# Attention scores of two heads in three 64-row passes instead of four 128-row passes, with the queries left on their partitions

## The chip, the core and the metric

The kernel runs on one core of one Trainium2 chip. The metric is the device time of one launch in microseconds (us); lower is better. The engines named below are TensorE (PE, with its weight loads as PEld), VectorE (DVE), ScalarE (ACT), GpSimd (POOL) and SyncE (SP), which issues nearly all DMAs here.

## What is computed

Two token groups (512 and 256 tokens, 768 together, width 1024, fp32) pass through two layers with shared weights. Layer 0 mixes tokens by windowed attention, layer 1 by a gated convolution; each layer then has a squared-ReLU MLP and a gated embedding. The change is in the attention of layer 0:

```python
qkv = h @ w_qkv                        # 16 query heads, 4 key heads, 64 wide each
# for each block of 128 queries, keys of the blocks before, of and after it:
logits = jnp.einsum('bqgrd,bkgd->bgrqk', qb, kb,
                    preferred_element_type=jnp.float32) * scale + band_bias
m = jnp.maximum(jnp.max(logits, axis=-1, keepdims=True), sink_logit)
pexp = jnp.exp(logits - m)
probs = pexp / (jnp.sum(pexp, axis=-1, keepdims=True) + jnp.exp(sink_logit - m))
return jnp.einsum('bgrqk,bkgd->bqgrd', probs, vb)
```

A block at the edge of its token group has 2 key blocks (256 keys), an inner one 3 (384 keys). The 512-token group has blocks with 2, 3, 3 and 2 key blocks, the 256-token group two with 2. Four query heads share one key head.

## The kernel before

All products keep fp32 accuracy with a rounded format: each operand is split into a high part in fp32r (ACT copies it, L779) and a low part (DVE subtracts, L782), and a product is the sum of high x high, high x low and low x high. `product` (L735) does so for the projections with three 128-row matmuls for each block of 128 inputs.

The attention stage is `mixer_attention` (L668 to L1333). Nothing in it is issued at once. Each step becomes an operation with an engine, a cost in us, the operations it waits for (`after`) and the buffers it uses. `Plan.order` (L544) then makes a list schedule: on each engine it takes, among the operations that can start, the one with the longest path behind it; it repeats this and keeps the best order. The costs are constants such as `MM` (L664), 0.2275, 0.1743 and 0.12 us for a matmul of 512, 384 and 256 columns. The engines then run their queues in that order, and semaphores hold the true dependences. Rings of buffers are operations too: an operation that opens a buffer waits for the users of the one before it in the ring. The score banks (tag `S`) are a ring of three PSUM banks (`BS`, L30).

Queries are made in eight units of 128 columns, that is two heads each (`queries`, L1031). A unit multiplies its weights with the normed tokens, scales the result (L1000), splits it into `qh` and `ql` with the two heads on partitions 0 to 63 and 64 to 127, and then four DMAs on SP's queue (L1045, issued at L694) move the halves: the tile of a head, one of eight slots (`QS`, L675), gets the high part on its upper 64 partitions and the low part on its lower 64. The keys (`keys`, L1014) are moved likewise, so that `khh[g]` holds the high part of key head g on both halves and `kll[g]` the low part on both.

Then `attend` (L1128) handles one key head and one block of queries, 24 times in all. For each of its four heads it takes one score bank and does two matmuls (L1153, L1154) of 128 rows: the head's high and low queries, one above the other, against `khh` and against `kll`. That gives all four products of the parts in two passes. DVE adds the bias, takes the minimum (the scores are negated) and writes the logits out of the bank (L1160); ACT takes the exponential and its sum (L1170). After the reciprocal (L1176) the rows are scaled (L1183 on ACT, L1185 on DVE), turned by PE (L1196), split (L1205, L1206) and multiplied with the values (L1211), and the result is joined (L1220, L1227).

The four groups of heads (L1237) are planned among the units of queries, the projections, and the output product (L1260), which fill PE while an attention step waits for DVE and ACT.

Of the kernel before, what the change touches and what calls it, by code (L numbers as in the profile page):

```python
# [10 lines left out]
F32 = mybir.dt.float32  # L11
F32R = mybir.dt.float32r
AF = mybir.ActivationFunctionType
ALU = mybir.AluOpType
# [3 lines left out]
P = 128  # L18
# [4 lines left out]
HEADS, KV, HD = 16, 4, 64  # L23
REP = HEADS // KV
# [5 lines left out]
BM, BS, BO, BT, BL = 1, 3, 1, 2, 5  # L30
# [20 lines left out]
def trunk_kernel(ctx: ExitStack, tc: tile.TileContext, a: dict, out: bass.AP):  # L51
    nc = tc.nc
    act, dve, pe = nc.scalar, nc.vector, nc.tensor
# [19 lines left out]
    nsink = const.tile([P, HEADS], F32, name="nsink")  # L73
# [105 lines left out]
    class Norm:  # L179


        n = T
# [30 lines left out]
        ready = False  # L213
# [268 lines left out]
    class Plan:  # L482
# [12 lines left out]
        def op(self, engine, cost, run, after=(), uses=(), behind=(), lands=None):  # L495
            flat = []
            for d in after:
                flat.extend(d if isinstance(d, (list, tuple)) else [d])
            o = Op(engine, cost, run, [d for d in flat if d is not None], list(behind), lands)
            for key in uses:  # L500
                assert key not in self.closed, key
                self.users.setdefault(key, []).append(o)
                if key in self.opened and self.opened[key] not in o.after:
                    o.behind.append(self.opened[key])
            self.ops.append(o)
            o.bonus = self.bonus if engine == "PE" else 0.0
            return o

        def new(self, tag, bufs, make):

            box = Box()
            box.key, box.free = self.ring(tag, bufs)
            box.make, box.ahead, box.op = make, self.last.get(tag), None
            self.last[tag] = box
            return box

        def first(self, box, engine, cost, run, after=(), uses=(), lands=None):

            def start():
                box.t = box.make()  # L520
                run()

            behind = [box.ahead.op] if box.ahead is not None and box.ahead.op is not None else []
            box.op = self.op(engine, cost, start, [box.free, *after], [box.key, *uses], behind, lands)
            self.opened[box.key] = box.op
            return box.op
# [135 lines left out]
        return 0.067 + 0.00104 * n  # L662

    MM = {512: 0.2275, 384: 0.1743, 256: 0.12}  # L664

    psum = ctx.enter_context(tc.tile_pool(name="ps", bufs=1, space=PSUM))

    def mixer_attention():  # L668
# [4 lines left out]
        odd = s1.enter_context(tc.tile_pool(name="odd", bufs=2))  # L673

        KHI, KLO, QS = (0, 1, 4, 8), (2, 3, 5, 9), (6, 7, 14, 15, 10, 11, 12, 13)  # L675
        W0 = SEQS[0]
        LW = 3 * P + 1
        plan = Plan()
        op, new, first = plan.op, plan.new, plan.first

        def bank(tag, name="mm"):
            return new(tag, PB[tag], lambda: psum.tile([P, 512], F32, tag=tag, name=name, bufs=PB[tag]))

        def temp(tag, name, dt=F32):
            return new(tag, 3, lambda: tmp.tile([P, T], dt, tag=tag, name=name, bufs=3))

        def place(i, name, dt=F32R):
            return new(f"S{i}", 1, lambda: slot(i, name, dt))

        def dma(box, src, n, after=(), uses=(), queue="SP", rate=400e3):  # L690

            def run():
                d, s = src()
                (nc.sync if queue == "SP" else act).dma_start(d, s)  # L694

            lands = n / rate
            if box is not None and box.op is None:
                d = first(box, queue, 0.46, run, after, uses, lands)
            else:
                d = op(queue, 0.46, run, after, uses, lands=lands)  # L700
            d.kind = "move" if rate < 400e3 else None
            return d
# [64 lines left out]
        def halves(w, xs, tags, col=0, fine=False):  # L767

            o, out = 0, []
            for tag, n in zip(tags, SEQS):  # L770
                ps = bank(tag)
                out.append((ps, o, n, product(ps, w, xs, o, n, col, fine)))
                o += n
            return out
# [215 lines left out]
        tr = first(rt, "PE", 0.4, columns, [rstd], [r.key])  # L990
        rcs = first(rc, "DVE", 0.1, lambda: dve.tensor_copy(rc.t[:], rt.t[:, : T // P]), [tr], [rt.key])

        def scaled(ps, t, neg, tag):

            ops = []
            for i, (b, o, n, last) in enumerate(ps):

                def run(b=b, o=o, n=n):
                    if neg:
                        dve.scalar_tensor_tensor(  # L1000
                            t.t[:, o : o + n], b.t[:, :n], -(HD**-0.5), r.t[:, o : o + n], ALU.mult, ALU.mult
                        )
                    else:
                        dve.tensor_tensor(t.t[:, o : o + n], b.t[:, :n], r.t[:, o : o + n], ALU.mult)

                f = first if i == 0 else lambda _, *z: op(*z)
                ops.append(f(t, "DVE", V(n), run, [last, rstd], [b.key, r.key] + ([t.key] if i else [])))
            hi, lo = temp(tag, "qh", F32R), temp(tag, "ql", F32R)
            h, l = split_op(hi, lo, lambda: t.t, T, ops, [t.key])
            return (hi, h), (lo, l)  # L1010

# [17 lines left out]
                        dst.ready.append(dma(dst, ends, 196608, [ready], [part.key] + ([dst.key] if i else []), rate=215e3))  # L1029

        def queries(c, w, tags, tag):  # L1031
            parts = scaled(halves(w, xs, tags), temp(tag, "qt"), True, tag)
            for j in range(2):
                h = 2 * c + j
                dst = qst[h] = place(QS[h % 8], "q")
                dst.ready = []
                for i, (part, ready) in enumerate(parts):

                    def ends(dst=dst, part=part, i=i, j=j):
                        return (  # L1040
                            dst.t[64 * i : 64 * i + 64, :].bitcast(F32),
                            part.t[64 * j : 64 * j + 64, :].bitcast(F32),
                        )

                    dst.ready.append(dma(dst, ends, 196608, [ready], [part.key] + ([dst.key] if i else []), rate=215e3))  # L1045

        wq = [prepared(fetched(a["w_q"][0]), KB)]
        skewed = dma(
# [79 lines left out]
        def attend(g, n, lo_blk, hi_blk):  # L1128
# [6 lines left out]
            mn = new("mn", 2, lambda: odd.tile([P, REP], F32, name="mn"))  # L1135
            sm = new("sm", 2, lambda: odd.tile([P, REP], F32, name="sm"))
            lg, sums = [], []
            for h in range(REP):
                hp, j = divmod(h, 2)
                H_ = REP * g + h  # L1140
                if j == 0:
                    L = new("L", BL, lambda: odd.tile([P, 2 * LW], F32, tag="L", name="L", bufs=BL).rearrange(
                        "p (a b) -> p a b", a=2))
                    lg.append(L)
                    sunk = first(L, "POOL", 0.2, lambda L=L, H_=H_: nc.gpsimd.tensor_copy(
                        L.t[:, :, 0:1], nsink[:, H_ : H_ + 2].rearrange("p (a b) -> p a b", b=1)), [turned])
                L = lg[hp]
                S = bank("S", "S")

                def score(S=S, H_=H_):  # L1150
                    q = qst[H_].t[:, n * P : (n + 1) * P]
                    kk = slice(k0 * P, k0 * P + w)
                    pe.matmul(S.t[:, :w], lhsT=q, rhs=khh_[g].t[:, kk], start=True, stop=False)  # L1153
                    pe.matmul(S.t[:, :w], lhsT=q, rhs=kll_[g].t[:, kk], start=False, stop=True)  # L1154

                s = first(S, "PE", 0.24 if nk == 2 else 0.35, score,
                          [qst[H_].ready, khh[g].ready, kll[g].ready], [qst[H_].key, khh[g].key, kll[g].key])

                def reduced(S=S, L=L, j=j, h=h, H_=H_, hp=hp):
                    dve.tensor_tensor_reduce(  # L1160
                        L.t[:, j, 1 : 1 + w], S.t[:, :w], bias[hp].t[:, j, j0 : j0 + w], 1.0,
                        nsink[:, H_ : H_ + 1], ALU.add, ALU.min, accum_out=mn.t[:, h : h + 1],
                    )

                args = "DVE", 0.40 if nk == 2 else 0.53, reduced, [s, bias[hp].ready, sunk, turned]
                uses = [S.key, L.key, bias[hp].key]
                m = first(mn, *args, uses) if h == 0 else op(*args, [mn.key, *uses])

                def exponent(L=L, j=j, h=h):
                    act.activation(L.t[:, j, : 1 + w], L.t[:, j, : 1 + w], AF.Exp, bias=mn.t[:, h : h + 1], scale=-1.0,  # L1170
                                   accum_out=sm.t[:, h : h + 1])

                args = "ACT", 0.50 if nk == 2 else 0.61, exponent, [m, sunk]
                e = first(sm, *args, [mn.key, L.key]) if h == 0 else op(*args, [sm.key, mn.key, L.key])
                sums.append(e)
            rs = op("DVE", 0.09, lambda: dve.reciprocal(sm.t[:], sm.t[:]), [sums], [sm.key])  # L1176
            normed = []
            for h in range(REP):
# [1368 lines left out]
```

## Time and profile before

| | us |
|---|---|
| median of 3 runs | 1637.23 (1636.72 to 1637.66) |
| profiled execution, its own time | 1636.62 |
| span of the profile, first to last instruction | 1634.8 |
| PE busy | 1623.9 |
| weight loads (PEld) busy | 1573.5 |
| DVE busy | 1390.6 |
| ACT busy | 918.9 |
| first and last score matmul, from the span's start | 71.0 and 232.5 |

The granted clock of TensorE is 0.999 of full speed. Busy times are those of one profiled execution; a matmul's recorded duration contains its latency, and neighbours overlap, so the step from start to start says what it occupies. In a row of a group stand the line, engine, operation, output and inputs, the shape and the count; behind the bar the busy time in us, the mean of one in ns, and the idle time before it with what ended it. A timeline row has its start and its length in us; "x2" merges two instructions that follow each other.

### The profile page before, as it was taken

How to read it: one execution, taken by the hardware profiler on the slowest of the kernel's cores; microseconds unless marked ns; L12 is line 12 of the kernel's file. 1: busy time of each engine (PE TensorE's matmuls, PEld its weight loads, DVE VectorE, ACT ScalarE, POOL GpSimd, SP SyncE). 2: the span in 40 equal slices, each digit the busy share in tenths (PEclk: the TensorE clock that was granted, in tenths of full speed). 3: DMA queues.
4: the chain of work that ended last, by engine and by line, in shares of the span. 5: the costliest groups of instructions: out<-in, count | busy, mean ns of one | idle time of the engine just before them, and what ended most of it. 6: DMA issues, size and time to landing. Idle time of an engine off the chain costs nothing.

```text
span 1634.8 us, 24125 instructions
## 1 busy us (share of the span) xinstructions
PE 1623.9 (99%) x9371; PEld 1573.5 (96%) x9371; DVE 1390.6 (85%) x2214; ACT 918.9 (56%) x1454; POOL 11.1 (1%) x60
## 2 busy tenths in 40 slices
PE   9999999999999999999999999999999999999998
PEld 7988889999999999999999999999999999999987
DVE  7579988999999989977878778778989999999686
ACT  7478876656555555545654334555555555654455
POOL 0000000000000000000000000000000000000000
PEclk9999999999999999999999999999999999999999
DMA  8744312322212122222312222211222121222332
GB/s 304 201 122 136 120 37 84 104 73 70 75 68 78 66 77 78 75 87 75 116 62 65 69 74 77 78 52 65 65 78 78 65 78 67 76 69 74 116 98 90
DMA packets 47822, 144.80 MB, mean 89 GB/s; under 512 B 6075, under 2 KB 9531, under 8 KB 47708
## 3 DMA queue, kind: packets, MB, share of 16 engines
q1 hardware_dynamic: 47564, 143.14, 27.0%
q8 instruction: 73, 1.20, 0.3%
q14 instruction: 41, 0.34, 0.1%
q10 hardware_dynamic: 144, 0.13, 0.0%
HBM read 123.85 MB, written 9.96 MB: 82 GB/s over the span
## 4 chain that ended last, share of the span: by engine, by line
PE 96%; DVE 1%; DMA 1%; ACT 1%; issue 0%; SPq 0%; DVEq 0%
PE a L470 34%; PE b L470 8%; PE mm L747 8%; PE mm L137 8%; PE p L1560 6%; PE d L470 5%; PE c L470 5%; PE gate L137 4%; PE gate L1894 4%; PE B L470 4%; PE C L470 4%; PE down L1894 2%; PE O L1211 1%; PE pt L1196 1%; PE S L1153 1%; PE S L1154 1%
## 5 line engine op out<-in xcount | busy, mean ns | idle before, releaser
L438 ACT ACTIVATE whi<-sum 128x1024 fp32r<-128x1024 f32 x66 | 70.0, 1061 | 253.9 <-PE a L470 252.2
L470 PE MATMUL a<-xs,whi 128*128 128x384 f32 x608 | 117.7, 334 | 0.0
L470 PEld LDWEIGHTS a<-xs,whi 128*128 128x128 f32 x608 | 106.5, 188 | 0.4 <-DVE t L2323 0.4
L470 PE MATMUL b<-t,zhi 128*128 128x384 f32 x528 | 106.6, 334 | 0.0
L470 PE MATMUL a<-t,zhi 128*128 128x384 f32 x528 | 106.6, 334 | 0.0
L470 PE MATMUL a<-t,whi 128*128 128x384 f32 x528 | 106.6, 334 | 0.0
L1716 DVE TENSOR_TENSOR x<-x,a 128x384 f32<-128x384 f32 x112 | 62.1, 554 | 51.4 <-PE a L470 51.4
L470 PE MATMUL a<-act,whi 128*128 128x384 f32 x448 | 95.6, 334 | 0.0
L470 PEld LDWEIGHTS b<-t,zhi 128*128 128x128 f32 x528 | 92.9, 188 | 0.0
L470 PEld LDWEIGHTS a<-t,zhi 128*128 128x128 f32 x528 | 92.9, 188 | 0.0
L470 PEld LDWEIGHTS a<-t,whi 128*128 128x128 f32 x528 | 92.9, 188 | 0.0
L438 ACT ACTIVATE zhi<-sum 128x1024 fp32r<-128x1024 f32 x66 | 69.8, 1057 | 40.8 <-DVE sum L414 26.1
L449 DVE TENSOR_TENSOR wlo<-wraw,whi 128x1024 fp32r<-128x1024 f32 x72 | 87.8, 1219 | 0.0
L438 ACT ACTIVATE whi<-wraw 128x1024 fp32r<-128x1024 f32 x72 | 75.6, 1051 | 19.5 <-issue 15.7
L449 DVE TENSOR_TENSOR zlo<-sum,zhi 128x1024 fp32r<-128x1024 f32 x66 | 80.4, 1217 | 0.7 <-ACT zhi L438 0.7
L747 PE MATMUL mm<-xs_mix,whi 128*128 128x512 f32 (+1 forms) x320 | 80.9, 340 | 0.0
L449 DVE TENSOR_TENSOR wlo<-sum,whi 128x1024 fp32r<-128x1024 f32 x66 | 80.5, 1220 | 0.0
L470 PEld LDWEIGHTS a<-act,whi 128*128 128x128 f32 x448 | 79.3, 188 | 0.0
L470 PE MATMUL a<-xs,wlo 128*128 128x384 f32 x304 | 64.9, 334 | 0.0
L470 PE MATMUL a<-t,zlo 128*128 128x384 f32 x264 | 60.9, 334 | 0.0
L470 PE MATMUL a<-t,wlo 128*128 128x384 f32 x264 | 60.9, 334 | 0.0
L470 PE MATMUL b<-t,zlo 128*128 128x384 f32 x264 | 60.9, 334 | 0.0
(396 smaller groups left out, 4477.6 us busy)
## 6 DMA issues: line engine op xcount, KB each, us to landing
wraw<-in_up SPq DMA_DIRECT2D x64, 512.0 KB, 3.4
wraw<-in_down SPq DMA_DIRECT2D x64, 512.0 KB, 3.5
wraw<-in_w_in SPq DMA_DIRECT2D x24, 512.0 KB, 3.5
wraw<-in_gate SPq DMA_DIRECT2D x16, 512.0 KB, 3.5
wraw<-in_w_q SPq DMA_DIRECT2D x8, 512.0 KB, 4.7
wraw<-in_w_out SPq DMA_DIRECT2D x8, 512.0 KB, 3.6
x_in<-in_x SPq DMA_DIRECT2D x8, 384.0 KB, 7.5
pj<-L SPq DMA_DIRECT2D x8, 384.0 KB, 5.1
```

The source lines that it names most:

```text
L137: pe.matmul(t, lhsT=w, rhs=x[:, o:e], start=first and i == 0 and j == 0, stop=last and i == n - 1 and j == 2)
L438: act.activation(hi[:], src, AF.Copy)
L449: dve.tensor_tensor(lo[:], src, hi[:].bitcast(F32), ALU.subtract)
L470: pe.matmul(ps, lhsT=a, rhs=b, start=start and i == 0, stop=i == len(terms) - 1, skip_group_check=True)
L747: pe.matmul(ps.t[:, :n], lhsT=a_, rhs=b_, start=k == 0 and j == 0, stop=k == len(xs) - 1 and j == 2,)
L1153: pe.matmul(S.t[:, :w], lhsT=q, rhs=khh_[g].t[:, kk], start=True, stop=False)
L1154: pe.matmul(S.t[:, :w], lhsT=q, rhs=kll_[g].t[:, kk], start=False, stop=True)
L1196: pe.transpose(pt.t[:, h * P : (h + 1) * P], lg[h // 2].t[:, h % 2, 1 + b * P : 1 + (b + 1) * P], ident[:],)
L1211: pe.matmul(O.t[:], lhsT=vb, rhs=part.t[:], start=b == 0 and i == 0, stop=b == nk - 1 and i == 1)
L1560: pe.matmul(ps[i][o], lhsT=wt[:, c], rhs=xs[f"x{h + 1}{1 + o}"][m][part], start=k == 0 and j == 0, stop=k == KB - 1 and j == 2,)
L1716: dve.tensor_tensor(t[:, o : o + H], t[:, o : o + H], f, op)
L1894: pe.matmul(ps.t[:, o : o + n], lhsT=a_, rhs=b_, start=begin and i == 0 and j == 0, stop=end and i == len(terms) - 1 and j == 2,)
```

## The change

A pair of heads is now scored together. `queries` no longer moves anything: the split writes the high part of the unit straight into one slot and the low part into another, with head 2c on partitions 0 to 63 and head 2c + 1 on partitions 64 to 127. `attend` takes two score banks for a pair. In each of three passes it issues two matmuls with 64 rows, one for each head and half: high queries with high keys, high queries with low keys, low queries with high keys. The product of the two low parts is left out, as in the projections. The planner prices a pair at three matmuls and a constant `SWITCH` of 0.1. The four keys' tiles, their moves, and all that follows the scores are as before.

```diff
     MM = {512: 0.2275, 384: 0.1743, 256: 0.12}
+    SWITCH = 0.1
...
-        def scaled(ps, t, neg, tag):
+        def scaled(ps, t, neg, tag, kept=None):
...
-            hi, lo = temp(tag, "qh", F32R), temp(tag, "ql", F32R)
+            hi, lo = kept or (temp(tag, "qh", F32R), temp(tag, "ql", F32R))
             h, l = split_op(hi, lo, lambda: t.t, T, ops, [t.key])
             return (hi, h), (lo, l)
...
         def queries(c, w, tags, tag):
-            parts = scaled(halves(w, xs, tags), temp(tag, "qt"), True, tag)
-            for j in range(2):
-                h = 2 * c + j
-                dst = qst[h] = place(QS[h % 8], "q")
...
-                    dst.ready.append(dma(dst, ends, 196608, [ready], [part.key] + ([dst.key] if i else []), rate=215e3))
+            kept = [place(QS[(2 * c + p) % 8], "q") for p in range(2)]
+            parts = scaled(halves(w, xs, tags), temp(tag, "qt"), True, tag, kept)
+            qst[c] = kept, [ready for _, ready in parts]
...
-            for h in range(REP):
-                hp, j = divmod(h, 2)
...
-                S = bank("S", "S")
-
-                def score(S=S, H_=H_):
-                    q = qst[H_].t[:, n * P : (n + 1) * P]
+            for hp in range(REP // 2):
...
+                Ss = [bank("S", "S") for _ in range(2)]
+                q, ready = qst[H0 // 2]
+
+                def score(Ss=Ss, q=q):
+                    Ss[1].t = Ss[1].make()
                     kk = slice(k0 * P, k0 * P + w)
-                    pe.matmul(S.t[:, :w], lhsT=q, rhs=khh_[g].t[:, kk], start=True, stop=False)
-                    pe.matmul(S.t[:, :w], lhsT=q, rhs=kll_[g].t[:, kk], start=False, stop=True)
+                    for i, (qt, kt) in enumerate(((q[0], khh_), (q[0], kll_), (q[1], khh_))):
+                        for j in range(2):
+                            rows = slice(HD * j, HD * j + HD)
+                            pe.matmul(
+                                Ss[j].t[:, :w],
+                                lhsT=qt.t[rows, n * P : (n + 1) * P],
+                                rhs=kt[g].t[rows, kk],
+                                start=i == 0,
+                                stop=i == 2,
+                            )
...
+                s = first(Ss[0], "PE", 3 * MM[w] + SWITCH, score, [Ss[1].free, ready, khh[g].ready, kll[g].ready],
+                          [Ss[1].key, q[0].key, q[1].key, khh[g].key, kll[g].key])
+                Ss[1].op = plan.opened[Ss[1].key] = s
+                for j in range(2):
+                    h, H_, S = 2 * hp + j, H0 + j, Ss[j]
...
```

The reduction and the exponential of each head stand in the last loop unchanged.

More of the change, by code (lines that the diff above doesn't have):

```diff
@@ L1031, in queries @@
         def queries(c, w, tags, tag):
-            parts = scaled(halves(w, xs, tags), temp(tag, "qt"), True, tag)
-            for j in range(2):
-                h = 2 * c + j
-                dst = qst[h] = place(QS[h % 8], "q")
[L1036 to L1043, printed above, removed]
-                    dst.ready.append(dma(dst, ends, 196608, [ready], [part.key] + ([dst.key] if i else []), rate=215e3))
+            kept = [place(QS[(2 * c + p) % 8], "q") for p in range(2)]
+            parts = scaled(halves(w, xs, tags), temp(tag, "qt"), True, tag, kept)
+            qst[c] = kept, [ready for _, ready in parts]
         wq = [prepared(fetched(a["w_q"][0]), KB)]
@@ L1137, in attend @@
             lg, sums = [], []
-            for h in range(REP):
-                hp, j = divmod(h, 2)
[L1140 to L1147, printed above, removed]
-                S = bank("S", "S")
-                def score(S=S, H_=H_):
-                    q = qst[H_].t[:, n * P : (n + 1) * P]
-                    kk = slice(k0 * P, k0 * P + w)
[L1153 to L1175, printed above, removed]
@@ new lines, in attend, with reduced, exponent @@
+            for hp in range(REP // 2):
+                H0 = REP * g + 2 * hp
+                L = new("L", BL, lambda: odd.tile([P, 2 * LW], F32, tag="L", name="L", bufs=BL).rearrange(
+                    "p (a b) -> p a b", a=2))
+                lg.append(L)
+                sunk = first(L, "POOL", 0.2, lambda L=L, H0=H0: nc.gpsimd.tensor_copy(
+                    L.t[:, :, 0:1], nsink[:, H0 : H0 + 2].rearrange("p (a b) -> p a b", b=1)), [turned])
+                Ss = [bank("S", "S") for _ in range(2)]
+                q, ready = qst[H0 // 2]
+                def score(Ss=Ss, q=q):
+                    Ss[1].t = Ss[1].make()
+                    kk = slice(k0 * P, k0 * P + w)
+                    for i, (qt, kt) in enumerate(((q[0], khh_), (q[0], kll_), (q[1], khh_))):
[13 more added lines that the diff above has]
+                    h, H_, S = 2 * hp + j, H0 + j, Ss[j]
+                    def reduced(S=S, L=L, j=j, h=h, H_=H_, hp=hp):
+                        dve.tensor_tensor_reduce(
+                            L.t[:, j, 1 : 1 + w], S.t[:, :w], bias[hp].t[:, j, j0 : j0 + w], 1.0,
+                            nsink[:, H_ : H_ + 1], ALU.add, ALU.min, accum_out=mn.t[:, h : h + 1],
+                        )
+                    args = "DVE", 0.40 if nk == 2 else 0.53, reduced, [s, bias[hp].ready, sunk, turned]
+                    uses = [S.key, L.key, bias[hp].key]
+                    m = first(mn, *args, uses) if h == 0 else op(*args, [mn.key, *uses])
+                    def exponent(L=L, j=j, h=h):
+                        act.activation(L.t[:, j, : 1 + w], L.t[:, j, : 1 + w], AF.Exp, bias=mn.t[:, h : h + 1], scale=-1.0,
+                                       accum_out=sm.t[:, h : h + 1])
+                    args = "ACT", 0.50 if nk == 2 else 0.61, exponent, [m, sunk]
+                    e = first(sm, *args, [mn.key, L.key]) if h == 0 else op(*args, [sm.key, mn.key, L.key])
+                    sums.append(e)
```

## The prediction

> **What bounds the kernel now.** I read the page first: its span, the line of busy tenths of PE and the chain that ended last.
>
> ```profile
> span 1634.8 us, 24125 instructions
> ...
> PE   9999999999999999999999999999999999999998
> ...
> PE 96%; DVE 1%; DMA 1%; ACT 1%; issue 0%; SPq 0%; DVEq 0%
> ```
>
> PE is busy in every slice and is 96% of the chain, so time is TensorE time. But a busy PE is a modelled one, and the change lies in the attention stage alone. So next comes the busy time of the engines in the stretch that holds all the scores, and then the waits of PE's two queues around it (matmuls are PE, weight loads are PEld).
>
> ```profile
> core 0: us, PE busy (x) PEld busy (x) DVE busy (x) ACT busy (x) POOL busy (x), PEclk, DMA share, GB/s
> 60.00:240.00 180.00, 179.49 (x1118) 158.06 (x1117) 153.69 (x422) 144.24 (x355) 9.32 (x43) 1.00 0.39 115
> ```
>
> ```profile
> engine line waited for: us in total, times, longest us
> PE S L1153 <- DVE mn L1160: 0.3, 1, 0.3
> PE pt L1196 <- ACT L L1183: 0.2, 1, 0.2
> ```
>
> ```profile
> PEld S L1153 <- DVE mn L1160: 2.0, 7, 0.6
> PEld mm L747 <- DVE xa L1265: 0.9, 2, 0.5
> ```
>
> The reader is to see three things. PE works 179.5 of 180 us at a granted clock of 1.00, and its matmuls wait 0.5 us in all. DVE (153.7) and ACT (144.2) are loaded but have room. The longest waits of the weight loads are for DVE, and none of these rows names a DMA. The planner fills every gap of the attention with projections, so the order may move without moving the time; what decides is how much PE time the scores take in all.
>
> **What the scores cost now.** Their groups in the same stretch, the count of each width, and the spacing of neighbours:
>
> ```profile
> L1160 DVE CUSTOM_DVE_ANT_0 L<-S,bias,nsink 128x256 f32<-128x256 f32 (+1 forms) x96 | 47.6, 523 | 3.0 <-PE S L1154 2.4
> ...
> L1153 PE MATMUL S<-kk,q 128*128 128x256 f32 (+1 forms) x96 | 30.1, 322 | 0.3 <-DVE mn L1160 0.3
> L1154 PE MATMUL S<-kk,q 128*128 128x256 f32 (+1 forms) x96 | 28.1, 300 | 0.0
> ```
>
> ```profile
> L1153 PE MATMUL S<-kk,q x96: 277/320/445, 71.0 to 232.3; 128*128 128x256 f32 x64, 128*128 128x384 f32 x32
> ```
>
> ```profile
> 110.47 0.28 PE L1153 MATMUL S<-kk,q 128*128 128x256 f32 x1
> 110.59 0.28 PE L1154 MATMUL S<-kk,q 128*128 128x256 f32 x1
> 110.71 0.28 PE L1153 MATMUL S<-kk,q 128*128 128x256 f32 x1
> ```
>
> ```profile
> 125.68 0.34 PE L1154 MATMUL S<-kk,q 128*128 128x384 f32 x1
> 125.86 0.34 PE L1153 MATMUL S<-kk,q 128*128 128x384 f32 x1
> 126.03 0.35 PE L1154 MATMUL S<-kk,q 128*128 128x384 f32 x1
> ```
>
> A matmul's own 0.28 us is latency; what it occupies is the step to the next start: 0.12 us at 256 columns, 0.175 at 384 (0.35 for two). There are 96 scores of two matmuls, 64 narrow and 32 wide: 128 x 0.12 + 64 x 0.175 = 15.4 + 11.2 = 26.6 us. The first matmul of a score is recorded longer than the second, 30.1 against 28.1 us over the 96, though both have the same shapes: 2.0 us of weight loads that came too late to hide, the size of the PEld wait above. So the scores take **28.6 us** of PE.
>
> **The streaming that goes.** A pair of heads had four passes of 128 rows and will have three, if the two 64-row matmuls of a pass run side by side: 48 pairs, 32 narrow and 16 wide, 96 x 0.12 + 48 x 0.175 = 11.5 + 8.4 = **19.9 us**. In the trace of before no two matmuls run side by side, so the bounds are 19.9 (fully) and 39.8 (six in a row). I take 19.9: the two matmuls share no rows, no weights and no bank.
>
> The Trainium skill ("TensorE: Matmul & The Clock Gate", Part 3: Packing small matmuls — row/col tiling) says that matmuls on different row groups start about 4 ns apart, and that four tiles of 32 rows were measured at 3.07x. No run here shows it yet; by a loss of that share (3.07 of 4) the sum would have some 6 us more.
>
> **The switching that comes.** All matmuls around the scores (projections, values, turns, products with V) use 128 rows. The trace has a few excursions to fewer rows. Three of them, loads and matmuls together:
>
> ```profile
> 41.79 0.28 PE L747 MATMUL mm<-xs_mix,wlo 128*128 128x256 f32 x1
> 41.99 0.19 PEld L988 LDWEIGHTS rt<-ident,rstd_mix 1*128 1x128 f32 x2
> 42.00 0.22 PE L988 MATMUL rt<-ident,rstd_mix 1*128 1x1 f32 x1
> ```
>
> ```profile
> 42.45 0.30 PEld L747 LDWEIGHTS mm<-xs_mix,whi 128*128 128x128 f32 x2
> 42.45 0.50 PE L747 MATMUL mm<-xs_mix,whi 128*128 128x512 f32 x1
> ```
>
> ```profile
> 19.29 1.09 PE L859 MATMUL bp<-oh,rbs 33*128 33x512 f32 x2
> 20.31 0.19 PEld L747 LDWEIGHTS mm<-p0h,wlo 128*128 128x128 f32 x1 [0.76 <-issue]
> 20.32 0.38 PE L747 MATMUL mm<-p0h,wlo 128*128 128x256 f32 x1
> 20.42 0.31 PEld L747 LDWEIGHTS mm<-p0h,whi 128*128 128x128 f32 x2
> ```
>
> ```profile
> 1584.75 0.38 PE L2122 MATMUL xt<-ident,x 128*128 128x128 f32 x2
> 1584.76 0.14 PEld L2122 LDWEIGHTS xt<-ident,x 128*128 128x128 f32 x1
> 1585.06 0.13 PEld L2124 LDWEIGHTS xt<-ident,rstd_ple 1*128 1x128 f32 x1 [0.17 <-issue]
> 1585.06 0.22 PE L2124 MATMUL xt<-ident,rstd_ple 1*128 1x1 f32 x1
> 1585.21 0.31 PEld L2122 LDWEIGHTS xt<-ident,x 128*128 128x128 f32 x3
> 1585.21 0.44 PE L2122 MATMUL xt<-ident,x 128*128 128x128 f32 x2
> ```
>
> In the last fence one matmul of one column stands between full ones. The full ones start 0.11 apart, so the last before it starts at 1584.86 and the second after it at 1585.21 + 0.44 - 0.27 = 1585.38: 0.52 us where two steps are 0.22. The excursion costs **0.30 us** and streams next to nothing. Its two halves look alike. The weight load is not done ahead; it starts 0.20 us after the start of the last full matmul (1584.86 to 1585.06, and 41.79 to 41.99), where a matmul would follow at 0.11 or 0.12, and on the way out the loader again idles on "issue" (0.76 after the 33 rows). I read this as an array that must run empty first. Then the load is itself in full view: 0.06 for these turns. For the weights of a product it is 0.11: two loads in a row at 42.45 and at 20.31 start 0.11 apart, and the narrow matmul at 20.32 is recorded at 0.38 and not 0.28. The scores and most of their neighbours have such weights, in and out: 0.30 + 2 x 0.05 = **0.40 us** an excursion. Both the 33 rows and the one row behave so; 64 rows I put with them. Bounds: 0 (half an array is switched for nothing) and 0.40; the nearest rows say 0.30 to 0.40.
>
> How many excursions? The ring of score banks has three, a pair takes two, so the next pair needs a bank that DVE must first reduce (523 ns by L1160). Two pairs cannot stand next to each other without PE idling, and the planner puts other work between: 48 excursions, 48 x 0.40 = **19.2 us**. The planner's own price for both ways is its constant 0.1.
>
> **The sum.** After: 19.9 + 19.2 = 39.1 us; before: 28.6. The 2.0 us of late loads goes, since a load behind a switch is in view anyway and is counted there. The difference is +10.5 us, on an engine that has nothing else to give.
>
> **What costs nothing.** The change removes the 32 moves of the queries.
>
> ```profile
> q<-qh SPq DMA_DIRECT2D x16, 192.0 KB, 3.1
> q<-ql SPq DMA_DIRECT2D x16, 192.0 KB, 3.6
> ```
>
> They are 6.3 MB and 3 to 4 us of latency each, hidden today: no PE row waits for them, and the projections cover them. SP's queue is shorter by 32 issues, so weights and biases may land earlier, for which PE does not wait either: 0, at most the 1 us of small waits above. New is that ACT (L779) and DVE (L782) write the query slots themselves, and have to wait until the scores of four units earlier have read them; behind ACT's wait would stand the exponentials, behind DVE's the reductions. The moves bore that wait so far, and the slots were plan-ordered by the same rule; 0, at most 1 us. ACT and DVE do the same instructions as before, on the same sizes. The planner will think a pair takes 0.46 or 0.62 us where I expect 0.76 or 0.93, so DVE and ACT run ahead of its plan and PE waits for them less, not more.
>
> **The forecast.** The profiled execution took 1636.6 us; 1636.6 + 10.5 = 1647.1. The median of the runs shown is 0.6 above it, so 1647.7 us. With 0.30 an excursion it is 4.8 less, 1642.9.
>
> **The rivals.**
> - *The switch is nearly free (the other side).* If loads for 64-row halves are done ahead across the switch, three passes simply replace four: up to 19.9 - 28.6 = -8.7, 1628.5 us; with the planner's 0.1 a pair, -3.9, 1633.3. It decides at (28.6 - 19.9) / 48 = 0.18 us an excursion: below it the kernel is faster. For it speaks only that 64 rows themselves are not in the trace; against it all the excursions above, the one with 33 rows too.
> - *The banks.* A pair waits for two of three banks. The seven waits of a load for DVE now are 0.29 us each (2.0 / 7); if half the 48 pairs waited so, +7: 1654.7. For it: the ring; against it: the planner knows the rule, and DVE has 26 us free in the stretch.
> - *The loads do not run side by side.* If the two halves' loads go one after the other at 0.11, a pass lasts 0.22 at either width: 48 x (0.66 + 0.40) = 50.9, +22.3: 1660.0. A load that cannot be done ahead of its own half's matmul would cost about the same, 0.11 + 0.12 a narrow pass. The rows of before have one load for one matmul, and cannot say.
> - *The matmuls do not run side by side,* so the change does not do what it says: 39.8 + 19.2 = 59.0, +30.4: 1668.1.
>
> The Trainium skill ("TensorE: Matmul & The Clock Gate", Part 3: Packing small matmuls — row/col tiling) states that a weight load overlaps with a running matmul only where the row group differs. In the trace it overlaps at equal rows too (of the scores above each follows the last at 0.12 with its own load), so I give this rule no more than a part of the third rival's chance.
>
> **How the numbers follow.** Forecast 0.55 (about 1641 to 1651); banks 0.10; serial loads 0.15; no side-by-side matmuls 0.07; free switch 0.13. The range reaches from 1639.0, a little below the 0.30 case, to 1662.0, past serial loads: it holds the first three, 0.80. It leaves out the cheap switch and the matmuls in a row. Within 0.2% (3.3 us, about what a measurement of this kernel tells from no change) lie the end of the cheap switches, 0.05; faster 0.09; slower 0.86.
>
> **What would show it.** In the profile after: two matmuls of 64 rows a few ns apart, six per pair, and passes 0.12 or 0.175 apart; a first load that starts about 0.2 us after the last full matmul; a load in view behind the last pass; PE still at 179 of 180 us; the attention ending some 10 us later; no q<-qh moves. Wrong it is if a 64-row load is done ahead under a 128-row matmul (then faster), if passes are 0.22 apart or single matmuls 0.12 apart (then slower still), or if PE rows show waits for L1160 of more than 5 us.

## The result and the profile after

The changed kernel takes 1643.97 us (median of 4, 1643.55 to 1644.38) against 1637.22 us before (1636.72 to 1637.66): a ratio of 1.0044, 95% interval 1.0032 to 1.0057, slower by 6.75 us. The profiled execution took 1643.55 us, 6.9 more than that of before.

From the page after, the span, PE's busy tenths, the chain, and the line of the DMA total:

```profile
span 1641.7 us, 24260 instructions
...
PE   9999999999999999999999999999999999999998
...
DMA packets 45262, 138.52 MB, mean 84 GB/s; under 512 B 5563, under 2 KB 9019, under 8 KB 45148
...
PE 97%; DVE 2%; ACT 0%; DMA 0%; issue 0%; SPq 0%; DVEq 0%; ACTq 0%
```

PE is still the whole of it. The moves are gone: 6.3 MB less than the 144.80 MB of before. Now the busy times in the same stretch of 60 to 240 us, and then the scores:

```profile
60.00:240.00 180.00, 180.00 (x1160) 144.56 (x1160) 146.12 (x396) 136.66 (x332) 9.40 (x43) 1.00 0.25 77
```

```profile
L1144 PEld LDWEIGHTS S<-kk,q x288: 182/185/187, 65.0 to 243.3; 64*128 64x128 f32 x144
L1144 PE MATMUL S<-kk,q x288: 273/331/442, 65.0 to 243.4; 64*128 64x256 f32 x96, 64*128 64x384 f32 x48
```

There are 288 matmuls of 64 rows, six for each of 48 pairs. The last starts at 243.4 us, where the last score of before started at 232.5. DVE did 146.1 us of work in the stretch and before 153.7: the attention is spread over a longer time. One pair in the timeline, matmuls and loads:

```profile
72.63 0.28 PE L748 MATMUL mm<-xs_mix,wlo 128*128 128x256 f32 x1
72.83 0.42 PEld L1144 LDWEIGHTS S<-kk,q 64*128 64x128 f32 x6
72.84 0.62 PE L1144 MATMUL S<-kk,q 64*128 64x256 f32 x6
...
73.39 0.19 PEld L748 LDWEIGHTS mm<-xs_mix,whi 128*128 128x128 f32 x1
73.39 0.50 PE L748 MATMUL mm<-xs_mix,whi 128*128 128x512 f32 x1
```

```profile
72.84 0.39 PE L1144 MATMUL S<-kk,q 64*128 64x256 f32 x2
```

This answers to the excursions of before. The first load starts 0.20 us after the start of the last full matmul. Six matmuls lie within 0.62 us, of which 0.28 is the latency of the last, so three passes start in 0.34: one load in view of 0.11, and two steps of 0.12, two matmuls at a time (in the second fence the two of the first pass together last 0.39, as long as one alone with its load in view, 0.38). The next load comes late again, 0.20 us after the start of the last pass, and the matmul with it is recorded at 0.50. All 48 excursions look like this one: the first load starts 0.20 to 0.21 us after the start of a full matmul of 256 columns or of a turn, and 0.32 to 0.33 us after one of 512 columns. That is each time some 0.09 us later than the full matmul's own step (0.12, 0.11 or 0.23 us); on the way out it is 0.20 to 0.21 us after a pass of 256 columns and 0.26 after one of 384, again 0.09 beyond the step. The waits of PE's loads name the same thing:

```profile
PEld S L1144 <- issue: 11.6, 38, 0.4
...
PEld S L1144 <- DVE mn L1159: 0.5, 2, 0.4
PEld vp L1070 <- DVE qt L1001: 0.4, 1, 0.4
```

"Issue" means that nothing in the records holds the load; that the change of row count does is what full_rows and twice show below. The scores' wait for DVE's reduction (mn) fell from 2.0 to 0.5 us. Some other late loads of the scores are put down to DVE in that view, but they are 0.2 to 0.4 us each, like those put down to "issue", and stand at the same change.

**Where the time came from.** As a mark behind the attention I take the first matmul of L470, in the MLP, which is the same in both kernels; first here before, then after:

```profile
L470 PE MATMUL a<-xs,whi x16: 334/334/334, 324.3 to 338.0; 128*128 128x384 f32 x16
```

```profile
L470 PE MATMUL a<-xs,whi x8: 334/334/334, 331.5 to 332.7; 128*128 128x384 f32 x8
```

All of the difference arises before it, 7.2 us, and none later (the spans differ by 6.9). I split the time up to there by steps, from the start of a matmul to that of the next. "Scores" are the steps that scores start; with pairs of 64 rows, the time from the start of the last full matmul ahead to the start of the second one behind, less what these two steps take in a steady stream (0.119, 0.174, 0.229 us for 256, 384, 512 columns, 0.109 for a turn). "Other" is what all other 128-row steps last beyond these values; some 3 us of it lie in the first 20 us of every kernel.

| kernel | time, us | first L470, us | scores | other |
|---|---|---|---|---|
| before | 1637.2 | 324.3 | 28.9 | 7.4 |
| after | 1644.0 | 331.5 | 38.6 | 5.0 |
| full_rows | 1633.0 | 320.9 | 22.3 | 10.8 |
| same_half | 1663.9 | 351.9 | 58.2 | 5.8 |
| twice | 1664.2 | 351.9 | 58.9 | 5.1 |
| moves_back | 1643.4 | 331.4 | 38.5 | 5.0 |
| four_heads | 1642.3 | 330.4 | 30.0 | 12.5 |
| four_banks | 1644.2 | 331.9 | 37.2 | 6.9 |
| before_pairs | 1635.5 | 322.8 | 27.9 | 6.9 |
| before_third | 1647.1 | 335.2 | 41.3 | 5.8 |
| price (0.4) | 1647.8 | 335.8 | 39.0 | 9.0 |
| price_02 | 1644.0 | 331.7 | 38.6 | 5.3 |
| price_00 | 1645.2 | 333.2 | 38.5 | 6.7 |

The last two columns add up to the third but for a constant of 288 us. The matmuls of PE stand in the same order in the changed kernel, full_rows, same_half and twice, and in the same order in before and before_third; the other kernels were planned anew. So the change cost 9.7 us in the scores, and the other waits came out 2.4 lower. A narrow pair takes 0.747 us, a wide one 0.915; three passes of 0.119 or 0.174 are 0.357 or 0.522 of that, and 0.39 is the two changes of row count, each some 0.09 us before the load and 0.11 of load in view.

### The profile page after: what moved, and what is told of

Its sections match the earlier page's. It is cut to its first block, busy times and chain, and to the rows that moved or that the text cites. A ratio compares the mean times of both kernels' runs of the same rounds, so it can differ in the third digit from the quotient of the medians.

```text
span 1641.7 us, 24260 instructions
## 1 busy us (share of the span) xinstructions
PE 1631.7 (99%) x9467; PEld 1566.4 (95%) x9467; DVE 1390.9 (85%) x2214; ACT 920.5 (56%) x1454; POOL 11.2 (1%) x60
## 4 chain that ended last, share of the span: by engine, by line
PE 97%; DVE 2%; ACT 0%; DMA 0%; issue 0%; SPq 0%; DVEq 0%; ACTq 0%
PE a L470 33%; PE mm L748 9%; PE b L470 8%; PE mm L137 6%; PE p L1559 6%; PE d L470 5%; PE c L470 5%; PE gate L137 4%; PE gate L1893 4%; PE B L470 4%; PE C L470 4%; PE down L1893 2%; PE S L1144 2%; PE O L1210 2%; PE pt L1195 2%; PE vp L1070 0%
## 5 line engine op out<-in xcount | busy, mean ns | idle before, releaser
L470 PE MATMUL a<-xs,whi 128*128 128x384 f32 x608 | 117.7, 334 | 0.0
L470 PEld LDWEIGHTS a<-xs,whi 128*128 128x128 f32 x608 | 106.4, 188 | 0.4 <-DVE t L2322 0.4
L470 PE MATMUL b<-t,zhi 128*128 128x384 f32 x528 | 106.6, 334 | 0.0
L470 PE MATMUL a<-t,zhi 128*128 128x384 f32 x528 | 106.6, 334 | 0.0
L470 PE MATMUL a<-t,whi 128*128 128x384 f32 x528 | 106.6, 334 | 0.0
L470 PE MATMUL a<-act,whi 128*128 128x384 f32 x448 | 95.6, 334 | 0.0
L470 PEld LDWEIGHTS b<-t,zhi 128*128 128x128 f32 x528 | 92.9, 188 | 0.0
L470 PEld LDWEIGHTS a<-t,whi 128*128 128x128 f32 x528 | 92.9, 188 | 0.0
L470 PEld LDWEIGHTS a<-t,zhi 128*128 128x128 f32 x528 | 92.9, 188 | 0.0
L470 PEld LDWEIGHTS a<-act,whi 128*128 128x128 f32 x448 | 79.3, 188 | 0.0
L470 PE MATMUL a<-xs,wlo 128*128 128x384 f32 x304 | 64.9, 334 | 0.0
L748 PEld LDWEIGHTS mm<-xs_mix,whi 128*128 128x128 f32 x320 | 53.5, 189 | 7.9 <-issue 1.5
L470 PE MATMUL b<-t,zlo 128*128 128x384 f32 x264 | 60.9, 334 | 0.0
L470 PE MATMUL a<-t,zlo 128*128 128x384 f32 x264 | 60.9, 334 | 0.0
```

Of the source, the lines that this page charges most:

```text
L470: pe.matmul(ps, lhsT=a, rhs=b, start=start and i == 0, stop=i == len(terms) - 1, skip_group_check=True)
L748: pe.matmul(ps.t[:, :n], lhsT=a_, rhs=b_, start=k == 0 and j == 0, stop=k == len(xs) - 1 and j == 2,)
```

## The experiments

**full_rows: the passes without the change of rows.**

```diff
-                    for i, (qt, kt) in enumerate(((q[0], khh_), (q[0], kll_), (q[1], khh_))):
-                        for j in range(2):
-                            rows = slice(HD * j, HD * j + HD)
-                            pe.matmul(Ss[j].t[:, :w], lhsT=qt.t[rows, ...], rhs=kt[g].t[rows, kk], start=i == 0, stop=i == 2)
+                    for j, qt, kt, i, e in ((0, q[0], khh_, 1, 0), (0, q[0], kll_, 0, 1), (1, q[1], khh_, 1, 1)):
+                        pe.matmul(Ss[j].t[:, :w], lhsT=qt.t[:, n * P : (n + 1) * P], rhs=kt[g].t[:, kk], start=i == 1, stop=e == 1)
```

> The changed kernel, but a pair's three passes are three matmuls of 128 rows (two into the first bank, one into the second) instead of six of 64 rows: the scores are other numbers, the streaming time of three passes stays and no matmul changes the row count. Theory (changing the row count costs 0.39 us a pair): 48 x 0.39 = 18.7 us less than the changed kernel, 1625, with up to 2.5 us of PE's small waits coming back: 1625 to 1628, so about 10 us below the kernel before. Rival (the time is lost to taking the banks in pairs, or to the new order): it stays at 1640 or above.

Measured: 1633.01 us, ratio to before 0.9978 (0.9969 to 0.9987). The scores' steps fell by 16.3 us, to 22.3, near the 18.7 that the theory wanted; the time fell by only 11.0 (the span by 10.5), since the other waits rose from 5.0 to 10.8. Waits of its loads (42 to 260 us):

```profile
PEld O L1208 <- DVE pl L1203: 3.1, 11, 0.5
PEld O L1208 <- ACT ph L1202: 1.9, 6, 0.5
PEld O L1208 <- ACT L L1167: 1.5, 3, 0.5
```

The products with V (O) now wait for DVE (pl) and ACT (ph) to split the turned tiles, and for an exponential of ACT (L1167). So the change of rows is what costs, and it is dearer than the whole gain; but the range of the theory, 1625 to 1628, was missed by 5 us: with 22.3 us of scores, PE is no longer alone the bound.

**same_half: both heads on one half of the array.**

```diff
-                            rows = slice(HD * j, HD * j + HD)
+                            rows = slice(0, HD)
```

> The changed kernel, but both matmuls of a pass use the lower 64 partitions (the second head's scores are computed from the first head's rows). Theory (the two halves run side by side, and only because they are different rows): six steps instead of three, 96 x 0.12 + 48 x 0.174 = 19.9 us more: 1662 to 1664. Rival (the two matmuls of a pass never overlapped in truth, only in the record): no change, 1644.

Measured: 1663.89 us, 19.9 above the changed kernel, where 19.9 was worked out. The pair in its timeline:

```profile
74.08 0.97 PE L1144 MATMUL S<-kk,q 64*128 64x256 f32 x6
```

0.97 against 0.62 is three more steps of 0.12. So two matmuls on different halves do run side by side, and they do so fully.

**twice: the change of rows doubled.**

```diff
+                        if i == 0:
+                            pe.matmul(Ss[1].t[:, :64], lhsT=q[0].t[:, n * P : (n + 1) * P],
+                                      rhs=khh_[g].t[:, k0 * P : k0 * P + 64], start=False, stop=False)
```

> The changed kernel with one more matmul of 128 rows and 64 columns after the first pass of each pair (it adds a wrong term to 64 columns of the second score), so that each pair leaves the 64-row mode and comes back: twice the changes of row count. Theory: 48 x (0.39 + 0.03) = 20 us more, 1662 to 1665. Rival (the cost of a pair is a wait for banks or a fixed cost of its first matmul): 48 x 0.03 to 0.13 = 1.5 to 6 us more, 1645 to 1650.

Measured: 1664.24 us, 20.3 above the changed kernel, or 0.42 a pair. A pair in its timeline:

```profile
73.42 0.38 PE L1144 MATMUL S<-kk,q 64*128 64x256 f32 x2
73.73 0.30 PE L1152 MATMUL S<-kk,q 128*128 128x64 f32 x1
73.96 0.50 PE L1144 MATMUL S<-kk,q 64*128 64x256 f32 x4
```

The small full matmul comes 0.31 after the first pass and the second pass 0.23 after that, where passes follow each other at 0.12. The cost goes with the number of changes, not with the pair: the added matmul takes no new bank and waits for no other engine. The rival of a wait for banks fell.

**moves_back: the moves without use.** After `qst[c] = ...`, four DMAs per unit from the query tiles into `qh` and `ql`:

```diff
+            for (part, ready), name in zip(parts, ("qh", "ql")):
+                dst = temp(tag, name)
+                for i in range(2):
...
+                    dma(dst, ends, 196608, [ready], [part.key] + ([dst.key] if i else []), rate=215e3)
```

> The changed kernel with the 32 moves of 192 KB issued again on the same queue, from the query tiles into tiles that nothing reads. Theory (the moves were hidden, and PE's small waits fell because PE got slower): no change, 1643.5 to 1644.8. Rival (the queue and the DMA engines that the change freed gave PE back about 2.4 us): 1646 or more.

Measured: 1643.41 us, ratio to before 1.0043 (1.0030 to 1.0055), as the changed kernel's, and 0.1 below the range that was expected. Its stretch from 60 to 240 us:

```profile
60.00:240.00 180.00, 180.00 (x1160) 144.79 (x1160) 145.89 (x396) 136.26 (x332) 9.70 (x43) 1.00 0.39 114
```

The DMA share is back at 0.39, as before the change, and the busy times of PE, DVE and ACT stay within 0.4 us of the changed kernel's. With the moves the planner's order differs in places. The moves are hidden in the changed kernel; leaving them out is worth nothing there.

**before_third: a slower PE without the change.**

```diff
-                    pe.matmul(S.t[:, :w], lhsT=q, rhs=kll_[g].t[:, kk], start=False, stop=True)
+                    pe.matmul(S.t[:, :w], lhsT=q, rhs=kll_[g].t[:, kk], start=False, stop=False)
+                    pe.matmul(S.t[:, :w], lhsT=q, rhs=kll_[g].t[:, kk], start=False, stop=True)
```

> The kernel before, its planned order and costs untouched, with the second matmul of each score issued twice (the product with the low keys is added twice): 64 x 0.12 + 32 x 0.174 = 13.2 us more of 128-row streaming, no change of row count, banks single, moves in place. Theory (PE's small waits fall by 2 to 3 us whenever PE gets that much slower): 10.2 to 11.5 us more than before, 1647 to 1648.5. Rival (the waits fell through the change's new order or its missing moves): the full 13.2, 1649.5 or more.

Measured: 1647.07 us against 1636.55 beside it, ratio 1.0063 (1.0048 to 1.0078): 10.5 us for 13.2 us of added work. In the table the scores rose by 12.4 (some of their late loads went) and the other waits fell by 1.6, from 7.4 to 5.8. Of the waits of the scores' loads for DVE, 2.0 us before, this is left:

```profile
PEld S L1153 <- DVE mn L1161: 0.4, 1, 0.4
```

The order of the operations is that of before, and so are the moves. So waits of PE can fall when PE has more to do, without a new order and without missing moves. That accounts for 1.6 of the 2.4 us of the changed kernel; the price runs below show that the order alone can make a difference of that size too. And it has an end: same_half and twice added some 20 us to the changed kernel in its own order, and the other waits did not fall below its 5.0 (5.8 and 5.1), so there the full 20 us were paid.

**before_pairs: the banks in pairs, at 128 rows.** In the kernel before, one step issues the four matmuls of two heads and takes two banks:

```diff
+                    for j in range(2):
+                        q = qq[j].t[:, n * P : (n + 1) * P]
+                        pe.matmul(Ss[j].t[:, :w], lhsT=q, rhs=khh_[g].t[:, kk], start=True, stop=False)
+                        pe.matmul(Ss[j].t[:, :w], lhsT=q, rhs=kll_[g].t[:, kk], start=False, stop=True)
...
+                s = first(Ss[0], "PE", 4 * MM[w], score, [Ss[1].free, qq[0].ready, qq[1].ready, khh[g].ready, kll[g].ready],
```

> The kernel before with its moves and its four passes of 128 rows, but two heads' scores issued as one step that takes two banks of three. Theory (pairing of the banks costs nothing that PE notices): 1636 to 1638.5. Rival (banks in pairs cost PE waits): 1640 to 1644.

Measured: 1635.51 us, ratio to before 0.9991 (0.9982 to 1.0), 0.5 below the range that was expected. Pairing the banks costs nothing; it may gain a trifle, but the interval touches 1, and the order is a new one. It is the lowest time of a kernel here that computes all the scores.

**four_heads: half as many changes of rows.** All four heads of a step are issued as one operation, with four score banks:

```diff
-BM, BS, BO, BT, BL = 1, 3, 1, 2, 5
+BM, BS, BO, BT, BL = 1, 4, 1, 1, 5
...
+            Ss = [bank("S", "S") for _ in range(REP)]
...
+                for hp, q in enumerate(qs):
+                    for i, (qt, kt) in enumerate(((q[0], khh_), (q[0], kll_), (q[1], khh_))):
...
+            s = first(Ss[0], "PE", 6 * MM[w] + 0.4, score,
```

> The changed kernel, but the four heads of a step are scored together, two pairs one right behind the other, so that there are 24 excursions to 64 rows instead of 48. It needs four score banks; the ring of the turned tiles gives one up (one bank instead of two). Theory (0.39 us an excursion): 24 x 0.39 = 9.4 us less than the changed kernel, 1634.5, with up to 3 us back for PE's small waits and the missing bank: 1634 to 1638. Rival (the cost grows with the matmuls of 64 rows, not with the changes of row count): 1643 or more.

**four_banks, its control:** the banks' numbers alone, with pairs.

> Control for four_heads: the changed kernel with its pairs, with four score banks and one bank for the turned tiles. Theory: 48 excursions as before, 1643 to 1646. If the banks were the matter (the wait of a pair for two of three), it would fall below 1641.

Measured: four_heads 1642.34 us, ratio 1.0035 (1.0021 to 1.0048); four_banks 1644.18 us, 1.0050 (1.0036 to 1.0064). The scores' steps did what the theory said, 38.6 to 30.0, or 0.36 for each of 24 excursions saved; the time did not, and lies between the ranges of theory and rival, because the other waits went from 5.0 to 12.5. The waits of four_heads' matmuls up to 310 us:

```profile
PE p L1566 <- DVE zlo L449: 2.2, 1, 2.2
PE O L1217 <- DVE heads L1233: 0.7, 1, 0.7
PE pt L1202 <- DVE pl L1212: 0.5, 1, 0.5
PE mm L748 <- DVE wlo L728: 0.4, 1, 0.4
```

All of these are waits for DVE: DVE is behind at the head of the MLP (p, 2.2 us, where the changed kernel waits 0.5) and in the attention; PE's loads wait for ACT as well. The one bank for turned tiles explains little by itself, as four_banks has it too, with 6.9. That control is not quite what was expected: its trace has 42 excursions and not 48, since with four banks two pairs stand right behind each other six times. There the second pair's passes follow at 0.12 to 0.18 us, without a gap between the pairs, and its scores take 37.2 and not 38.6. How much of the rest is the four heads' coming at once and how much the planned order, these runs do not tell apart.

**price, price_02, price_00: the planner's constant.**

```diff
-    SWITCH = 0.1
+    SWITCH = 0.4
```

> The changed kernel with the planner's constant for a pair at 0.4 instead of 0.1, which is what the trace shows; only the planned order can change. Theory (PE's work is the same and it waits for little): 1643 to 1645. Rival (the wrong price sent PE into waits): 1641.5 or less.

> The changed kernel with the planner's constant for a pair at 0.2. Only the planned order can change. If the planner's order carries a scatter of its own of some us (theory since the run at 0.4 came out 4 us slower), this lies anywhere from 1641 to 1648, with the excursions at 38 to 39 us as ever. Rival (a higher price itself makes the order worse): between 1644 and 1648, about 1645.3.

> The changed kernel with the planner's constant for a pair at 0.0. Scatter of the order: anywhere from 1641 to 1648, the excursions at 38 to 39 us. Rival (a lower price makes the order better): 1643 or less.

Measured: 1645.16 at 0.0, 1643.97 at 0.1, 1644.01 at 0.2, 1647.83 at 0.4. The scores take 38.5 to 39.0 us in all four; the other waits make the difference. At 0.4 the matmuls wait for DVE at the head of the MLP, and the loads of the products with V wait for it in the attention:

```profile
PE p L1559 <- DVE zlo L449: 1.5, 1, 1.5
PE O L1210 <- DVE pl L1205: 0.3, 1, 0.3
```

```profile
PEld O L1210 <- DVE pl L1205: 2.3, 8, 0.5
```

My expectation that an honest price would change nothing fell: it was 3.9 us worse. Nor is there a trend: 0.0 is dearer than 0.1 and 0.2. The order that the planner finds carries some us of its own, which no price here predicts: the other waits are 5.0, 5.3, 6.7 and 9.0 for the same work. Differences of 2 to 4 us between kernels with differently planned orders are to be read with that in mind, the 2.4 us between before and after among them.

## Why the prediction held, point by point

- **The bound.** Right in the main: the whole difference arose in the attention and just behind it, on a full PE. But the 0.5 us of waits that it read are those of the matmuls' rows alone. By the table PE lost 7.4 us to other waits up to the MLP, and this is the part that moved.
- **The streaming.** Right: a pass of two 64-row matmuls takes the step of one 128-row matmul. same_half paid the 19.9 us that this saves. The Trainium skill ("TensorE: Matmul & The Clock Gate", Part 3: Packing small matmuls — row/col tiling) gave matmuls on different row groups that start about 4 ns apart, and 3.07x for four tiles, from which a loss of some 6 us was estimated. The trace agrees with the first: the records of the two matmuls of a pass mostly start 3 to 4 ns apart. It shows nothing of the loss for two tiles of 64 rows: a pass takes 0.12 us, the step of one 128-row matmul.
- **The switching.** Right in its parts and its size: the late load (0.20 us after the last start), 48 excursions, 0.39 us each where 0.40 was worked out from the excursion of a single column and the loads of a product. The 0.76 us behind the 33 rows say less than they seem to: the streaming of those matmuls lies in them. full_rows shows that the change of rows is the cost, and twice confirmed the size with 0.42 for another excursion with 64 columns. That the array must first run empty is a reading: the traces show the late load, not its reason. The Trainium skill ("TensorE: Matmul & The Clock Gate", Part 3: Packing small matmuls — row/col tiling) has the rule that a load overlaps with a running matmul only where the row group differs. The trace does not agree: the six loads of a pair lie within 0.42 us in all, so those of the second pass run while the first streams on the same rows. The rival of loads in a row fell too, as passes are 0.12 us apart and not 0.22.
- **The sum.** The scores were to go from 28.6 to 39.1, +10.5; they went from 28.9 to 38.6, +9.7.
- **What failed in size.** The step "DVE and ACT run ahead of its plan and PE waits for them less, not more" was entered as nothing, and the other waits came out 2.4 us lower (7.4 to 5.0). With the 0.8 of the scores this is nearly all of the distance from 1647.7 to 1644.0. The sign was in part luck. before_third shows a fall of 1.6 us in an unchanged order when PE gets slower; but the planner's order moves these waits as much: at a price of 0.4, with the same scores, they were 9.0, above those of before, and the kernel took 1647.8 us. The reason that the prediction gave, a planner that thinks a pair too cheap, stays open: the waits are lower at 0.1 and 0.2 than at an honest 0.4, but at 0.0 they rise again, to 6.7.
- **The moves.** Right: moves_back shows no difference. The writes into the query slots, entered at 0 to 1 us, show no wait for the scores in the trace after.
- **The rivals.** Banks: before_pairs shows no cost. A free switch: full_rows came to 1633.0, not 1628.5, so this rival was priced too low: where PE saves time, part of it is met by waits for DVE and ACT, 5.8 of 16.3 us from the changed kernel to full_rows. The break-even of 0.18 us an excursion was not tested; at 0.39 the change loses 6.75 us, and without the change of rows it gains some 4. Two of the rivals' times were added up 0.5 us too high: from 1637.2, +22.3 gives 1659.5 and +30.4 gives 1667.6. Neither bears on the forecast.

## What to carry to other kernels

Before splitting the array for a few small matmuls, count the changes of row count: here the way in and out cost 0.39 us together, more than the one pass of 0.12 or 0.17 us that a pair saved, and any full matmul between two such blocks pays it again. Price it from excursions that the kernel already has, even one of a single column. And on an engine that is full, work that is removed gains less once its neighbours are nearly full too: 16.3 us removed gained 11.0. Work that is added comes out smaller only while there are waits that it can take up: 13.2 us added to the kernel before cost 10.5, but 20 added to the changed kernel cost 20.

## What was not expected of the hardware

The two halves' loads and matmuls ran without any loss against each other: a 64-row pass took 0.119 us for two matmuls of 256 columns. And the excursion to 64 rows behaves like that of one column: both ways there are 0.09 us between the last step and the next load, and then the load in view. The difference between 0.30 and 0.39 us is that of the loads, 0.06 for a turn's and 0.11 for a product's; that the price depends on nothing else was not tested beyond these kinds of excursion.
